# Head norms' statistics in two-block pieces between products, key parts on other engines and in other steps

## The chip, the core and the metric

The kernel runs on one core of a Trainium2 chip. The core has TensorE (PE: matrix products; PEld is the load of a product's stationary operand), VectorE (DVE), ScalarE (ACT), GpSimd (POOL) and SyncE (SP, which issues most transfers). Each engine works through its own queue in order. The metric is the device time of one execution in microseconds (us).

## The reference

Two layers of a decoder trunk over 1024 tokens of width 1024, all float32: a gated short convolution and then sliding-window attention, each followed by a SwiGLU channel mixer. The change lies in the attention layer:

```python
qkv = h @ w_qkv
q = rmsnorm(q, q_gain)      # per head of 64, over 16 query heads
k = rmsnorm(k, k_gain)      # per head of 64, over 4 key heads
scores = einsum(qb, kw) * scale          # 128 queries against 256 keys
scores = where(mask, scores + alibi, -inf)
p = softmax(concat([scores, sink]))[..., :-1]
out = einsum(p, vw)
return out @ w_o
```

## The kernel before

Float32 accuracy is made from a high part (float32r) and a low part (the rest): each product of two matrices is three matrix products, high by high, high by low, low by high. The projections to queries and keys use a seven-product scheme: each pair of 128-column blocks is made from seven sums of products (kinds 0 to 6), and each kind is 12 matmuls of 128x512 (four steps p of three). "Seven kinds of the keys" (numbers j = 0 to 6 in `seq`) are followed by seven of the first query pair (j = 7 to 13); all 14 are run by `first_pairs` before the attention. The remaining query pairs are run piecemeal inside the attention by `work_of_pairs`.

After its last kind a block of raw keys or queries (two heads by 1024 tokens, in a tile of 128 x 1024) is normed. ACT squares it in two halves (`squares`, L2011 for keys, L2134 for queries). PE then sums the squares over each head: `head_stats` (L1678) is one matmul for each 128 tokens, 128 columns of squares as the stationary operand against two columns of ones, so eight for a block of 1024 tokens; as float32 each is two loads and two matmuls in the trace, 16 in all. Their 16 columns go to one PSUM bank. From it DVE makes the mean (`head_mean`, L1685), ACT takes a logarithm and an exponential (L1697, L1702), DVE refines it (L1704 to L1711), ACT or POOL spreads the 16 columns to 128 x 512 (`spread`, L1803), PE turns those (`turn_blocks`, L1808, four matmuls), and DVE multiplies them in (L2036 for keys, L1813 for queries). The bank named P3 serves the statistics and every turn in `first_pairs`; there is one buffer of it, so a turn waits until DVE has read the one before.

The normed keys are then laid out as scores need them: `part(g, e, i)` for key block g and head e makes in four steps a high part (i = 0, ACT, L1873), its copy on the other 64 partitions (i = 1, DVE, L1875), a low part (i = 2, raw minus high, POOL, and DVE for g, e = 0, 0 alone; L1878), and its copy (i = 3, ACT, L1880). Each works on 64 x 1024 elements. The values are scaled and split by `keep_v` (ACT L1794, DVE L1796).

The attention runs in steps, one for 128 tokens of one pair of heads. Within a step the order is written as a string, `ORDER = "SPTMEDkPHLVOPK"`: scores of block n (S; PE, L2231 and L2232, into the bank P0, of which there is one), row extremes (M; DVE, L2246, which read P0), exponentials (E; ACT, L2266, block n-1), turn (T; PE, L2274, block n-2), high and low part of the turned block (H, ACT, L2281; L, DVE, L2287), values (V; PE, L2300, block n-3), their keeping (O; ACT L2318, DVE L2319), and at each P a piece of the products L1997 of a later query pair. At k and K the helpers run that `plan(d, f)` has put d steps ahead: an integer d at K (end of the step), a half at k. `keep_q` plans the norm of one query block in this way: squares at 1 and 1.5, statistics and mean at 2.5, log and refinement at 3, spreading from 3, turns at 4.5 and 5.5. A turn T uses the banks P1 and P3 by turns, and the statistics sit in the one that the next T will take. In `first_pairs` the order is set by a list of due times instead: `line.work` puts PE's work in a row, and `at(t, f)` puts another engine's step at a planned time.

## Time and profile before

| | us |
|---|---|
| median of 3 runs | 1926.59 |
| the runs | 1924.79, 1926.59, 1926.68 |
| the profiled execution, its own time | 1926.32 |
| its span in the trace | 1924.2 |
| PE busy | 1913.0 (99%) |
| DVE, ACT, POOL busy | 1327.0, 893.7, 303.8 |
| chain that ended last, share of PE | 95% |

A line of the timeline merges equal instructions in a row; the start of the next line, not the length, tells how long a group held PE, since PE's matmuls overlap. The stretches that matter lie between 975 us (the first key product) and 1060 us (the attention's twelfth step).

### The profile page before, as it was taken

The page shows a single profiled execution, that of the slowest core. Times are in us where ns is not written, and L with a number is a line of the kernel's source. Part 1 is how long each engine was busy: PE and PEld are TensorE (multiplying, and loading weights), DVE is VectorE, ACT ScalarE, POOL GpSimd, SP SyncE. Part 2 cuts the span into 40 slices and gives each one's busy share as a digit, 9 for nine tenths or more (in the row PEclk, how much of TensorE's full clock was granted, in tenths as well). Part 3 has the DMA queues.
Part 4 walks back from the last instruction along what each step waited for, and adds up shares of the span by engine and source line. Part 5 has one row for each costly group of instructions (what it writes and reads, how often), then busy time and mean ns, then how long its engine had stood idle before and what let it go on. Part 6 is the DMA issues. An engine that isn't in the chain of part 4 may idle for free.

```text
span 1924.2 us, 25416 instructions
## 1 busy us (share of the span) xinstructions
PE 1913.0 (99%) x9045; PEld 1597.5 (83%) x9045; DVE 1327.0 (69%) x2295; ACT 893.7 (46%) x1753; POOL 303.8 (16%) x389
## 2 busy tenths in 40 slices
PE   9999999999999999999999999999999999999999
PEld 8888888888888888888887888888888888888887
DVE  8997877975655666555867987788756665665543
ACT  5543464633333334444557787655333333344441
POOL 0001131011111100000014556310111111100000
PEclk9999999999999999999999999999999999999999
DMA  8896595388898637986364661232675575467563
GB/s 315 260 259 155 117 248 160 112 273 216 221 251 234 154 136 288 320 255 209 105 255 146 210 213 54 89 142 81 218 210 142 197 194 162 131 244 275 197 228 100
DMA packets 154910, 374.13 MB, mean 194 GB/s; under 512 B 15392, under 2 KB 26784, under 8 KB 154784
## 3 DMA queue, kind: packets, MB, share of 16 engines
q1 hardware_dynamic: 119392, 263.16, 39.8%
q0 software_dynamic: 35248, 109.33, 23.1%
q8 instruction: 71, 1.16, 0.2%
q14 instruction: 55, 0.45, 0.1%
q10 hardware_dynamic: 144, 0.03, 0.0%
HBM read 300.89 MB, written 149.42 MB: 234 GB/s over the span
## 4 chain that ended last, share of the span: by engine, by line
PE 95%; DVE 2%; ACT 2%; issue 1%; POOL 0%; DVEq 0%; ACTq 0%; POOLq 0%
PE acc L1004 16%; PE acc L1007 16%; PE acc L1005 16%; PE P L1004 10%; PE P L1005 10%; PE P L1007 10%; PE acc L172 2%; PE P L1997 2%; PE acc L1997 2%; PE acc L176 1%; PE P L2274 1%; PE P L1678 1%; PE acc L1137 1%; PE acc L1139 1%; PE acc L1138 1%
## 5 line engine op out<-in xcount | busy, mean ns | idle before, releaser
L1004 PE MATMUL acc<-XS,G 128*128 128x512 f32 x926 | 360.4, 389 | 0.0
L1005 PE MATMUL acc<-XS,G 128*128 128x512 f32 x926 | 360.2, 389 | 0.0
L1007 PE MATMUL acc<-XS,G 128*128 128x512 f32 x926 | 360.2, 389 | 0.0
L1004 PE MATMUL P<-A,G 128*128 128x512 f32 x550 | 214.1, 389 | 0.0
L1007 PE MATMUL P<-A,G 128*128 128x512 f32 x550 | 214.0, 389 | 0.0
L1005 PE MATMUL P<-A,G 128*128 128x512 f32 x550 | 214.0, 389 | 0.0
L1007 PEld LDWEIGHTS acc<-XS,G 128*128 128x128 f32 x926 | 173.8, 188 | 36.1
L1004 PEld LDWEIGHTS acc<-XS,G 128*128 128x128 f32 x926 | 173.8, 188 | 36.1
L1005 PEld LDWEIGHTS acc<-XS,G 128*128 128x128 f32 x926 | 173.8, 188 | 35.9
L1004 PE MATMUL acc<-A,G 128*128 128x512 f32 x442 | 172.1, 389 | 0.0
L1007 PE MATMUL acc<-A,G 128*128 128x512 f32 x442 | 172.0, 389 | 0.0
L1005 PE MATMUL acc<-A,G 128*128 128x512 f32 x442 | 171.9, 389 | 0.0
L938 DVE TENSOR_TENSOR G<-WL,G 128x512 fp32r<-128x512 f32 x168 | 115.0, 685 | 73.1 <-ACT G L937 73.1
L938 DVE TENSOR_TENSOR G<-WR,G 128x512 fp32r<-128x512 f32 (+1 forms) x216 | 144.2, 668 | 30.7 <-ACT G L937 30.6
L937 ACT CAST G<-WR 128x512 fp32r<-128x512 f32 (+1 forms) x216 | 130.5, 605 | 68.8 <-PE acc L1007 24.6
L937 ACT CAST G<-WH 128x512 fp32r<-128x512 f32 (+1 forms) x174 | 104.7, 602 | 83.8 <-PE acc L1007 38.1
L938 DVE TENSOR_TENSOR G<-WH,G 128x512 fp32r<-128x512 f32 (+1 forms) x174 | 115.5, 664 | 21.6 <-ACT G L937 21.6
L1339 ACT ACTIVATE G<-G 128x512 f32<-128x512 f32 x88 | 55.8, 634 | 159.4 <-DVE G L1436 153.1
L1007 PEld LDWEIGHTS P<-A,G 128*128 128x128 f32 x550 | 103.2, 188 | 21.5
L1004 PEld LDWEIGHTS P<-A,G 128*128 128x128 f32 x550 | 103.2, 188 | 21.4
L1005 PEld LDWEIGHTS P<-A,G 128*128 128x128 f32 x550 | 103.2, 188 | 21.4
L901 POOL DMA_DIRECT2D s<-s x68 | 60.0, 893 | 351.7 <-DMA s<-s 169.6
(414 smaller groups left out, 3797.9 us busy)
## 6 DMA issues: line engine op xcount, KB each, us to landing
G<-h SPq DMA_DIRECT2D x70, 512.0 KB, 4.5
s<-in_w_dn SPq DMA_DIRECT2D x32, 704.0 KB, 8.4
h<-X POOLq DMA_DIRECT2D x44, 512.0 KB, 5.7
s<-s POOLq DMA_DIRECT2D x32, 704.0 KB, 6.9
WR<-s SPq DMA_DIRECT2D x79, 256.0 KB, 4.0
WR<-in_w_gu SPq DMA_DIRECT2D x36, 512.0 KB, 5.5
WH<-in_w_gu SPq DMA_DIRECT2D x36, 512.0 KB, 4.6
XS<-q_ops SPq DMA_DIRECT2D x36, 512.0 KB, 5.0
```

Of the source, the lines that this page charges most:

```text
L172: pe.matmul(ps.half(h), wh, xs[:, j, c], start=first and j == 0, stop=False)
L176: pe.matmul(ps.half(h), wl, xs[:, 0, c], start=False, stop=last)
L901: nc.gpsimd.dma_start(dst[to], dst[of], accum_op=ALU.add)
L937: lambda: act.copy(out_hi, raw),
L938: lambda: lo_eng.tensor_tensor(out_lo, raw, plain(out_hi), ALU.subtract),
L1004: pe.matmul(ps, w[:, 0, c], x[:, 0, :], start=start and e == 0, stop=False, skip_group_check=True)
L1005: pe.matmul(ps, w[:, 0, c], x[:, 1, :], start=False, stop=False, skip_group_check=True)
L1007: pe.matmul(ps, w[:, 1, c], x[:, 0, :], start=False, stop=last, skip_group_check=True)
L1137: pe.matmul(ps, hi[:, kc], xs[:, 0, c], start=k == 0, stop=False, skip_group_check=True)
L1138: pe.matmul(ps, hi[:, kc], xs[:, 1, c], start=False, stop=False, skip_group_check=True)
L1339: state["silu"] = act.activation(x, x, AF.Silu)
L1997: pe.matmul(ps, g[:, w, c], x[:, b, :], start=begin and i == 0, stop=end and i == 2, skip_group_check=True)
```

## The change

Three things change. First, `head_stats` is called for two or four blocks of 128 tokens instead of eight: for the two key blocks and the first query block in four pieces of two, each behind three or six products; for the seven later query blocks in two pieces of four, one at k and one at K of the same step, and the mean goes to K, log, refinement and the first spread half a step later. The second turn of the second key block goes from behind one group of six products to behind the next. Second, of the four key parts, the copy of the high part (i = 1) goes from DVE to ACT (but for the first), the low part (i = 2) from POOL to DVE, and parts 1 to 3 start a step or half a step later. Third, the last two blocks of values are scaled in step 3 instead of step 0. Lines after the change are up to five higher than before (L1878 is L1879, L2036 is L2038, L2246 is L2251).

```diff
@@ part
                 if i == 0:
                     act.copy(hi[rows, e, :], raw[rows, :])
+                elif i == 1 and (g, e) == (0, 0):
+                    dve.tensor_copy(hi[rest, e, :], raw[rows, :])
                 elif i == 1:
-                    dve.tensor_copy(hi[rest, e, :], raw[rows, :])
+                    act.copy(hi[rest, e, :], raw[rows, :])
                 elif i == 2:
-                    eng = dve if (g, e) == (0, 0) else pool
-                    eng.tensor_tensor(lo[rows, e, :], raw[rows, :], plain(hi[rows, e, :]), ALU.subtract)
+                    dve.tensor_tensor(lo[rows, e, :], raw[rows, :], plain(hi[rows, e, :]), ALU.subtract)
@@ first_pairs
-            def stats(g):
-                s["st", g] = bank("P3")
-                head_stats(s["st", g], s["side", g], 0, NB)
+            def stats(g, b):
+                if ("st", g) not in s:
+                    s["st", g] = bank("P3")
+                head_stats(s["st", g], s["side", g][:, b * P : (b + 2) * P], b, 2)
...
+                    if (j, p) in ((5, 1), (5, 2), (5, 3), (6, 0)):
+                        stats_work(0, 2 * (p - 1) % NB)
                     if p == 1 and j == 7:
                         rows_work(0, 0)
-                    if p == 1 and j == 8:
-                        stats_work(1)
-                    if p == 1 and j == 10:
-                        rows_work(1, 1)
-                    if p == 1 and j == 12:
-                        line.work(4, first.stats)
-                        for d, f in ((0.1, first.mean), (0.5, first.guess), (0.9, first.newton), (1.2, first.wide0), (2.9, first.wide1)):
+                    if (j, p) in ((8, 1), (8, 2), (8, 3), (9, 0)):
+                        stats_work(1, 2 * (p - 1) % NB)
+                    if j == 10 and p in (1, 3):
+                        rows_work(1, p // 2)
+                    if (j, p) in ((11, 2), (11, 3), (12, 1), (12, 2)):
+                        line.work(1, first.stats, {(11, 2): 4, (11, 3): 6, (12, 1): 0, (12, 2): 2}[j, p])
+                    if (j, p) == (12, 2):
+                        for d, f in ((0.1, first.mean), (0.3, first.guess), (0.5, first.newton), (0.65, first.wide0), (2.9, first.wide1)):
...
-                if j == 5:
-                    stats_work(0)
-                if j in (7, 9):
-                    rows_work(*{7: (0, 1), 9: (1, 0)}[j])
+                if j == 7:
+                    rows_work(0, 1)
...
-            for pair in (0, 1):
-                at(t + 0.1, keep_v, 1, pair)
+            at(t + 0.1, keep_v, 1, 0)
@@ keep_q
-                (1.5 + first, [stats_of, mean]),
-                (2 + first, [guess, newton]),
-                (rows[0] - 1.5, [lambda: wide_of(0)]),
+                (1.5 + first, [lambda: stats_of(0, 4)]),
+                (2 + first, [lambda: stats_of(4, 4), mean]),
+                (2.5 + first, [guess, newton, lambda: wide_of(0)]),
@@ the attention's steps
-            for d, g, e in ((4, 0, 1), (6.5, 1, 0), (8, 1, 1)):
-                for i, dd in enumerate((0, 0, 0.5, 3.5 if g == 0 else 3)):
+            plan(3, lambda: keep_v(1, 1))
+            for d, g, e in ((5, 0, 1), (7, 1, 0), (8.5, 1, 1)):
+                for i, dd in enumerate((0, 0.5, 1, 3 if g == 0 else 2.5)):
```

DVE's queue at the norm of the second key block (raw keys G_1164), before the first query product's sums (L1979): the first key part's cast and subtraction and the multiplication by the turned factors. Before:

```order
L1711 SCALAR_TENSOR_TENSOR hr_y_8238<-hr_t_8244,hr_y_8238 128x16
L1875 CAST A_1177_8272<-G_1161_8073 64x1024
L2036 SCALAR_TENSOR_TENSOR G_1164_8153<-G_1164_8153,cst_61,P_1175_8265 128x512
L1878 TENSOR_TENSOR A_1178_8273<-G_1161_8073,A_1177_8272 64x1024
L2036 SCALAR_TENSOR_TENSOR G_1164_8153<-G_1164_8153,cst_61,P_1179_8285 128x512
L1979 TENSOR_TENSOR G_1176_8270<-P_1145_7852,G_1176_8270 128x512
```

After the change the same place of DVE's queue reads:

```order
L1711 SCALAR_TENSOR_TENSOR hr_y_8250<-hr_t_8256,hr_y_8250 128x16
L1875 CAST A_1176_8269<-G_1161_8073 64x1024
L1879 TENSOR_TENSOR A_1177_8270<-G_1161_8073,A_1176_8269 64x1024
L2038 SCALAR_TENSOR_TENSOR G_1164_8156<-G_1164_8156,cst_61,P_1178_8278 128x512
L2038 SCALAR_TENSOR_TENSOR G_1164_8156<-G_1164_8156,cst_61,P_1179_8292 128x512
L1980 TENSOR_TENSOR G_1175_8267<-P_1145_7852,G_1175_8267 128x512
```

The subtraction (L1878, now L1879) stood between the two multiplications of the second key block; now it stands ahead of both.

DVE's queue at the attention's first two steps: scaled values (L1796), a weight's split (L1940, L1941) and the row extremes of the first scores (L2246). Before:

```order
L1796 SCALAR_TENSOR_TENSOR A_1192_8402<-acc_7900,r_7999,A_1192_8402 128x4x64 x2
L1796 SCALAR_TENSOR_TENSOR A_1192_8402<-acc_7949,r_7999,A_1192_8402 128x4x64 x2
L1940 CAST WL_7846<-WR_7842 128x512
L1941 TENSOR_TENSOR WL_7846<-WR_7842,WL_7846 128x512
L2246 ISA s_1188_8369,mx_8468<-P_1201_8461,cst_61 128x64
L2246 ISA mx_8468 128x1
L2246 ISA s_1188_8369,mx_8468<-P_1201_8461,cst_61 128x128
L2246 ISA mx_8468 128x1
L1875 CAST A_1177_8272<-G_1161_8073 64x1024
```

After the change DVE's queue reads there:

```order
L1796 SCALAR_TENSOR_TENSOR A_1192_8402<-acc_7900,r_7999,A_1192_8402 128x4x64 x2
L1941 CAST WL_7846<-WR_7842 128x512
L1942 TENSOR_TENSOR WL_7846<-WR_7842,WL_7846 128x512
L1796 SCALAR_TENSOR_TENSOR A_1192_8402<-acc_7949,r_7999,A_1192_8402 128x4x64 x2
L2251 ISA s_1188_8369,mx_8468<-P_1201_8461,cst_61 128x64
L2251 ISA mx_8468 128x1
L2251 ISA s_1188_8369,mx_8468<-P_1201_8461,cst_61 128x128
L2251 ISA mx_8468 128x1
L1941 CAST WL_7847<-WR_7842 128x512
L1942 TENSOR_TENSOR WL_7847<-WR_7842,WL_7847 128x512
```

The second pair of scaled values now stands behind the split, still ahead of the first extremes; the key part's cast behind the extremes is gone.

DVE's queue some steps on, from the turned block's low part (L2287) over the extremes of the fourth scores to the mean of the next query block (L1685). Before:

```order
L2287 TENSOR_TENSOR G_1208_8518<-P_1207_8508,G_1208_8518 128x256
L1940 CAST WL_7846<-WR_7842 128x512
L2246 ISA s_1188_8369,mx_8468<-P_1209_8527,cst_61 128x192
L2246 ISA mx_8468 128x1
L2246 ISA s_1188_8369,mx_8468<-P_1209_8527,cst_61 128x192
L2246 ISA mx_8468 128x1
L1875 CAST A_1211_8543<-G_1164_8153 64x1024
L1685 SCALAR_TENSOR_TENSOR hr_m_8556<-P_1213_8547,eps_r_8000 128x16
L2287 TENSOR_TENSOR G_1216_8561<-P_1210_8534,G_1216_8561 128x512
L2319 TENSOR_TENSOR G_1218_8567<-P_1217_8564,G_1218_8567 64x2x2x64
```

After the change the same steps of DVE's queue read:

```order
L2292 TENSOR_TENSOR G_1208_8517<-P_1207_8506,G_1208_8517 128x256
L1879 TENSOR_TENSOR A_1177_8270<-G_1161_8073,A_1176_8269 64x1024
L1941 CAST WL_7846<-WR_7842 128x512
L2251 ISA s_1188_8369,mx_8468<-P_1209_8527,cst_61 128x192
L2251 ISA mx_8468 128x1
L2251 ISA s_1188_8369,mx_8468<-P_1209_8527,cst_61 128x192
L2251 ISA mx_8468 128x1
L2292 TENSOR_TENSOR G_1212_8549<-P_1210_8534,G_1212_8549 128x512
L2324 TENSOR_TENSOR G_1214_8555<-P_1213_8552,G_1214_8555 64x2x2x64
L1685 SCALAR_TENSOR_TENSOR hr_m_8568<-P_1211_8543,eps_r_8000 128x16
```

A subtraction of a key part (L1879) now stands ahead of the extremes of the fourth scores, a cast behind them is gone, and the mean now stands behind the low part and the kept values instead of ahead of them.

## Rows read from the trace of the kernel before

**Rows 1.** Page, part 1: busy us (share), instructions of each engine.

```profile
PE 1913.0 (99%) x9045; PEld 1597.5 (83%) x9045; DVE 1327.0 (69%) x2295; ACT 893.7 (46%) x1753; POOL 303.8 (16%) x389
```

**Rows 2.** PE timeline, products before the attention: start, us, engine, line, operation, out<-in, count.

```profile
992.08 1.84 PE L1678 MATMUL P<-cst,G 128*128 128x2 f32 x16
...
993.78 2.34 PE L1997 MATMUL P<-A,WH 128*128 128x512 f32 x9
...
998.01 0.60 PE L1808 MATMUL P<-cst,G 128*128 128x128 f32 x4
...
998.36 1.63 PE L1997 MATMUL P<-XS,G 128*128 128x512 f32 x6
...
1007.56 0.60 PE L1808 MATMUL P<-cst,G 128*128 128x128 f32 x4
...
1013.93 1.52 PE L1997 MATMUL P<-A,WL 128*128 128x512 f32 x6
...
1015.54 1.95 PE L1678 MATMUL P<-cst,G 128*128 128x2 f32 x16
```

**Rows 3.** Windows: length, busy us of PE, PEld, DVE, ACT, POOL; clock; DMA; GB/s.

```profile
1017.40:1021.20 3.80, 3.80 (x11) 2.98 (x11) 1.16 (x6) 2.05 (x6) 0.00 (x0) 0.55 0.00 0
...
1032.00:1040.00 8.00, 6.11 (x39) 5.13 (x39) 6.82 (x23) 5.25 (x17) 2.61 (x2) 1.00 0.74 272
...
1040.00:1060.00 20.00, 19.20 (x127) 16.34 (x127) 16.45 (x49) 18.53 (x50) 14.04 (x10) 1.00 0.26 79
```

**Rows 4.** DVE timeline, same stretch; in brackets idle before it, releaser.

```profile
1008.20 0.75 DVE L2036 SCALAR_TENSOR_TENSOR G<-G,cst,P 128x512 f32<-128x512 f32 x1 [0.15 <-PE P L1808]
...
1009.33 1.22 DVE L1878 TENSOR_TENSOR A<-G,A 64x1024 fp32r<-64x1024 f32 x1 [0.38 <-ACT A L1873]
...
1017.52 0.17 DVE L1685 SCALAR_TENSOR_TENSOR hr_m<-P,eps_r 128x16 f32<-128x16 f32 x1 [0.40 <-PE P L1678]
```

**Rows 5.** ACT timeline, same stretch.

```profile
1008.24 1.05 ACT L1873 CAST A<-G 64x1024 fp32r<-64x1024 f32 x1
...
1014.85 0.63 ACT L2134 ACTIVATE G<-G 128x512 f32<-128x512 f32 x1 [1.33 <-DVE G L1981]
...
1018.99 0.62 ACT L1803 COPY G<-hr_y 128x512 f32<-128x512 f32 x1 [0.80 <-DVE hr_y L1711]
```

**Rows 6.** PE timeline of the attention's first steps: the rows with a wait.

```profile
1032.85 0.36 PE L2231 MATMUL P<-A,G 128*128 128x192 f32 x1 [2.25 <-DVE mx L2246]
...
1035.98 0.36 PE L2231 MATMUL P<-A,G 128*128 128x192 f32 x1 [1.04 <-DVE mx L2246]
...
1044.86 0.36 PE L2231 MATMUL P<-A,G 128*128 128x192 f32 x1 [0.19 <-DVE mx L2246]
...
1049.60 0.63 PE L1808 MATMUL P<-cst,G 128*128 128x128 f32 x4 [0.18 <-DVE G L2287]
...
1054.57 0.30 PE L2231 MATMUL P<-A,G 128*128 128x64 f32 x1 [0.43 <-POOL G L2169]
```

**Rows 7.** DVE timeline around the attention's first scores.

```profile
1027.44 1.65 DVE L1796 SCALAR_TENSOR_TENSOR A<-acc,r,A 128x256 fp32r<-128x256 f32 x4
...
1029.53 2.67 DVE L1941 TENSOR_TENSOR WL<-WR,WL 128x512 fp32r<-128x512 f32 x1
...
1032.83 1.05 DVE L1875 CAST A<-G 64x1024 fp32r<-64x1024 f32 x1
```

**Rows 8.** POOL timeline, same stretch as Rows 7.

```profile
1026.87 1.29 POOL L2169 TENSOR_TENSOR G<-G,G 64x512 fp32r<-64x512 f32 x1 [1.69 <-ACT G L2164]
...
1029.27 2.39 POOL L1878 TENSOR_TENSOR A<-G,A 64x1024 fp32r<-64x1024 f32 x1 [1.11 <-ACT A L1873]
```

**Rows 9.** View of line L1875 from 985 to 1180: durations min/median/max in ns.

```profile
L1875 DVE CAST A<-G x4: 689/1000/1648, 1006.4 to 1046.0; 64x1024 fp32r<-64x1024 f32 x4
```

**Rows 10.** Timeline of PE and DVE behind the fourth query block's statistics.

```profile
1085.70 0.62 PE L1997 MATMUL acc<-WH,WL 128*128 128x512 f32 x2
...
1086.52 0.43 DVE L2319 TENSOR_TENSOR G<-P,G 64x256 f32<-64x256 f32 x1
```

More of the change, by code (lines that the diff above doesn't have):

```diff
@@ L2045, in of_product, with stats_work @@
                 all_of(three(j, p, x))
-            def stats_work(g):
-                line.work(4, stats, g)
+            def stats_work(g, b):
+                line.work(1, stats, g, b)
                 t = line.end
+                if b < NB - 2:
+                    return
                 at(t + 0.1, log, g)
@@ L2134, in squares, with stats_of @@
                 act.activation(t["side"][h], t["raw"][:, h * 512 : h * 512 + 512], AF.Square)
-            def stats_of():
-                t["st"] = bank(pos["free"])
-                for h in (0, 1):
-                    head_stats(t["st"], t["side"][h], 4 * h, 4)
+            def stats_of(b0, n):
+                if "st" not in t:
+                    t["st"] = bank(pos["free"])
+                for b in range(b0, b0 + n, 2):
+                    head_stats(t["st"], t["side"][b // 4][:, b % 4 * P : (b % 4 + 2) * P], b, 2)
             def mean():
@@ L2178, in keep_q @@
                     squares0=lambda: squares(0),
-                    stats=stats_of,
+                    stats=lambda b: stats_of(b, 2),
                     mean=mean,
```

## Prediction, made before the changed kernel ran

> **What bounds the kernel now.** I read the page first: PE is busy for 1913.0 us, 99% of the span [rows 1], so any gain must come from time in which PE waits, runs slower or does work of another kind. Then I went through PE's timeline for starts that come later than the work before them explains, from the first key product (975 us) to the end of the attention's first twelve steps (1060 us), where all moved instructions stand. There are three kinds.
>
> The first is the statistics. Sixteen loads and matmuls hold PE from 992.08 to 993.78, 1.70 us, although their matmuls have two columns [rows 2]: one load each, 0.106 us. Ten blocks are normed in this way.
>
> The second is one slow stretch. The first query block's statistics start at 1015.54. The six products from 1013.93 show 1.52, with the last one 0.39 long, so one starts (1.52 - 0.39) / 5 = 0.227 after another, and the next start was due at 1015.29; ACT's squares end at 1014.85 + 0.63 = 1015.48 [rows 2, 5]: a wait of 0.25 us. Right behind these statistics the granted clock is 0.55 for 3.80 us [rows 3], that is 1.2 GHz for nearly all of it and 2.4 GHz elsewhere. At full clock its work takes 3.80 x 0.55 = 2.09, so 1.71 us are lost. What PE did before it fell is the wait and then 1.7 us of two-column matmuls. From 1032 to 1060, with one more such block, it is 1.00 [rows 3].
>
> The third is waits in the attention: 2.25, 1.04, 0.19, 0.18 and 0.43 us [rows 6]. The first has its cause in DVE: a subtraction of 128x512 takes 2.67 us and ends 0.54 us after a POOL subtraction of 2.39 us does [rows 7, 8]. DVE stood still while POOL ran; its own work is near the 0.54. The 1.04 has the key part's cast (1.05) in the way of the next extremes [rows 7].
>
> **The change part by part.** The sum is made against the profiled execution, 1926.32 (2.1 over its span, 0.27 below the median of 1926.59).
>
> *Pieces, PE's own time: 0.* A turn of four matmuls also has four loads, and already stands between products: 0.35 us from 998.01 to 998.36, and the six products behind it last 1.63, about 0.1 over their usual [rows 2]. So four loads cost 0.45 and four pieces 1.8, what one row of sixteen costs with its own 0.1. Bounds: -0.9 (three quartered blocks at 4 x 0.35 against 1.70) to +0.2. The Trainium skill, "TensorE: Matmul & The Clock Gate", section "Architectural detail: the array is 16x 32x32, not 1x 128x128", says that PE can pull weight loads ahead of matmuls in flight. By it the loads of a piece could all hide behind the products beside them; that is the last rival below.
>
> *The wait of 0.25 and the slow clock: -0.25 and -1.71.* In four pieces no more than 0.45 us of two-column work stand together, with 0.7 to 1.4 us of products between. I take the whole; bound 0, if the clock falls elsewhere.
>
> *Second turn of the second key block: +1.08, new.* DVE's subtraction (1.22) now stands ahead of both multiplications. It waits for ACT's part of 64x1024, which started at 1008.24 and took 1.05 [rows 5]; ACT now spreads factors first, 0.53 to the next start (0.62 long) [rows 5], so the part ends near 1009.80, the subtraction runs to 1011.05 [rows 4], and the first multiplication (0.75) to 1011.72. The turned factors of the second half need the same bank P3. PE ends the product before at 1007.56 [rows 2], runs six products (1.36), the first turn (0.44) and six products, and wants the second turn near 1010.7. It gets the bank near 1011.77. Bounds 0 (if ACT or DVE gets there a microsecond earlier) to 1.3.
>
> *Two follow-on waits: +0.23 and +0.27.* From 1011.77 on the multiplication, the kept sum and the squares (0.63) follow each other and end near 1014.45; PE asks for the first piece at 1014.25. The last piece then ends near 1018.96. From the mean's start to the end of the spread before were 1017.52 to 1018.99 + 0.62 = 2.09 [rows 4, 5], with 0.17 for the way to DVE, so 1021.22; PE is at the turn at 1021.0. Here the old order had 1.7 us to spare. Bounds 0 to 0.8.
>
> *First scores: the wait goes from 2.25 to 1.28, -0.97.* POOL no longer has its 2.39 in the way, but its third low part of the queries (1.29) [rows 8] moves up into that place, and starts as DVE comes to the cast and subtraction. So I let DVE stand about 1.2 us again instead of 2. The second pair of scaled values still runs ahead of the extremes (four took 1.65) [rows 7]. Bounds: -2.15 (no meeting) to 0.
>
> *Steps 4 to 12: +0.6.* The waits there were 1.84 (1.04 + 0.19 + 0.18 + 0.43). ACT was idle 2.75 us of the 8 and 1.47 of the 20 [rows 3], 4.22 together; it gets three casts and one first part more in there, 4 x 1.05 = 4.2. It is full, so the stretch can't become shorter by what DVE gives back. DVE loses three casts (0.69 at their shortest [rows 9]; up to 1.05 as they ran) and gets three subtractions of 1.22: 3.66 - 2.07 = +1.59, or +0.97 by casts that waited. Each stands ahead of the extremes of the next scores or of the multiplication that frees a turn's bank, and PE has one bank for scores. DVE had 28 - 23.27 = 4.73 us idle [rows 3], so not all of it lands on the path: two thirds of 0.97. ACT's logarithm now waits for the mean behind a later statistics half, with casts around it, which fills the same 4.22. Bounds: -1.84 (every wait gone) to +2.9 (1.59 and one POOL operation of 1.29 in the way).
>
> *Later blocks (seven in halves): 0.* Two halves hold as many loads. DVE's and ACT's work there is the same, and stands in a step with no statistics wait in the trace. The new tie is a rival.
>
> Sum: -0.25 - 1.71 + 1.08 + 0.50 - 0.97 + 0.60 = -0.75, so 1925.57, 0.05% below the median before. About 0.2%, 3.85 us, is what a measurement of this kernel can tell from no change: 1922.7 to 1930.4.
>
> **The rivals.**
>
> *The queues take the new work.* ACT and DVE were idle for 4.2 and 4.7 us in the stretch, and a due-time order may meet well: no new turn waits, DVE never meets POOL, all 1.84 gone: -0.25 - 1.71 - 2.15 - 1.84 = -5.95, 1920.4. Against it: ACT has nothing left, and three waits would have to vanish together. Half of it gives 1922 to 1923.
>
> *The mean holds up the turn.* With the statistics at K, the next T takes their bank and must wait until DVE has read the mean. Behind the fourth block: products end at 1085.70 start plus 0.46, then half the statistics 0.88, scores 0.45, one product 0.23, so T at 1087.72; DVE's kept values end at 1086.95 [rows 10], the mean follows the statistics (1087.04) near 1087.4. 0.3 us to spare: it decides where DVE is later than that. With one low part and one kept block more ahead (0.69 + 0.43) T waits 0.8; seven blocks, 5.6: 1925.57 + 5.6 = 1931.2, slower. For it: DVE was busy 23.27 of 28 us. Against: nothing but the mean moved there, and low parts may start earlier, since ACT no longer waits for 1.7 us of statistics first.
>
> *The clock is not given back.* A wait of 1.08 between two turns may bring the low clock as 0.25 and statistics did: 1925.57 + 1.71 = 1927.3, no change. For it: the timed runs before differ by 1.8, about one such stretch, so it comes in some executions and not in others.
>
> *The pieces' loads hide behind the products* (the rule above): ten blocks of 1.70, 17 us, 1909. Against: the turn of four loads at 998.01 still costs 0.35 [rows 2].
>
> **How the numbers follow.** Forecast 0.57 (1924 to 1927); queues take the work 0.20; the mean holds up the turn 0.07; the clock is not given back 0.15; loads hide 0.01. Faster: most of the first rival, and the last: 0.18. Slower: most of the second: 0.06. Same: 0.76. The range leaves out the better half of the first rival and the second: 1921.9 to 1928.2.
>
> **What would show it.** Right: no window below clock 1.00 near 1017; statistics in groups of four with starts 0.45 apart from their products; a PE wait near 1 us at the second key block's second turn, on DVE; a first scores wait of 1 to 1.5; ACT busy over 95% from steps 4 to 10, and PE waits of 2 to 3 us in sum there, on DVE. Wrong: no wait at that turn, or less than 1 us of waits in steps 4 to 12 (then 1920 to 1923); turns that wait for a mean in the later blocks (then 1928 and more).

## The result, and the profile of the changed kernel

The changed kernel takes 1929.52 us (median of 12, 1928.79 to 1934.50); the kernel before takes 1926.09 beside it (12, 1924.79 to 1927.14). The medians are 3.43 us (0.18%) apart. The ratio is 1.0023, 95% interval [1.0014, 1.0032]; it lies nearer to that of the means (1930.62 and 1926.11) than to that of the medians. So the kernel is slower clear of noise, by about the 0.2% that the prediction named as its limit. The ratios here and below leave out three disturbed executions of later runs (2751.55, 3910.2 and 4834.2 us). Forecast were 1925.57 and 1921.9 to 1928.2. The profiled execution took 1929.86, its span 1928.1.

First the page's part 1 and then four windows of the changed kernel, with the columns of [rows 1] and [rows 3]:

```profile
PE 1915.2 (99%) x9045; PEld 1598.3 (83%) x9045; DVE 1326.9 (69%) x2295; ACT 896.5 (46%) x1756; POOL 296.8 (15%) x386
```

```profile
1017.00:1021.00 4.00, 4.00 (x23) 3.33 (x21) 1.66 (x7) 1.74 (x6) 0.00 (x0) 1.00 0.00 0
...
1040.00:1047.00 7.00, 6.57 (x25) 5.82 (x26) 5.12 (x16) 4.71 (x14) 2.16 (x3) 0.53 0.11 39
1047.00:1060.00 13.00, 11.02 (x71) 8.92 (x69) 11.43 (x30) 11.91 (x27) 4.85 (x4) 1.00 0.14 50
...
1032.00:1060.00 28.00, 25.17 (x143) 21.05 (x141) 21.23 (x59) 24.10 (x55) 7.29 (x7) 0.88 0.33 115
```

There is no slow clock near 1017 [rows 3]. A longer one stands in the attention: 0.53 of full speed from 1040 to 1047. The stretch behind it has PE idle for 2 us of 13, though its clock is full. PE's timeline has the waits, those of the key products first:

```profile
1011.65 0.63 PE L1808 MATMUL P<-cst,G 128*128 128x128 f32 x4 [0.91 <-DVE G L2038]
...
1031.33 0.36 PE L2236 MATMUL P<-A,G 128*128 128x192 f32 x1 [1.15 <-DVE mx L2251]
...
1036.90 1.05 PE L1678 MATMUL P<-cst,G 128*128 128x2 f32 x8 [0.20 <-DVE G L2292]
...
1040.43 0.50 PE L2236 MATMUL P<-A,G 128*128 128x192 f32 x1 [0.65 <-DVE mx L2251]
...
1054.10 0.63 PE L2279 MATMUL P<-cst,G 128*128 128x128 f32 x4 [0.98 <-DVE WH L1813]
...
1055.24 0.38 PE L2305 MATMUL P<-G,A 128*128 128x256 f32 x1 [0.28 <-ACT G L2286]
1055.96 0.38 PE L2306 MATMUL P<-G,A 128*128 128x256 f32 x1 [0.34 <-DVE G L2292]
...
1057.43 0.27 PE L2236 MATMUL P<-A,G 128*128 128x64 f32 x1 [0.38 <-DVE mx L2251]
```

The same work can be followed through both traces (times from the span's start):

| place on PE | before | after | gained or lost since the row above | the prediction's terms for it |
|---|---|---|---|---|
| first key product | 975.73 | 975.44 | | |
| first scores | 1028.85 | 1028.43 | -0.13 | -0.25 - 1.71 + 1.08 + 0.50 = -0.38 |
| next scores, which have the wait of 2.25 in [rows 6] | 1032.85 | 1031.33 | -1.10 | -0.97 |
| first scores of the second query block | 1054.57 | 1057.43 | **+4.38** | +0.60 |
| scores of a later step | 1154.62 | 1157.85 | +0.37 | 0 |
| end of the span | 1924.2 | 1928.1 | +0.67 | 0 |

The first two stretches came out near the forecast; the third decides, with steps 4 to 12. But the -0.13 is luck in good part. Seven of the experiments below (e2, e7, e9, e10, e11, e14 and e15) have the first three norms just as the kernel before has them. In their traces PE is busy for the same 13.91 us from 1010 to 1024, and the clock is full in all seven. The kernel before, then e11:

```profile
1010.00:1024.00 14.00, 13.91 (x64) 11.29 (x64) 7.10 (x16) 8.32 (x17) 3.42 (x9) 0.88 0.31 106
```

```profile
1010.00:1024.00 14.00, 13.91 (x73) 11.50 (x73) 7.23 (x17) 9.73 (x21) 4.61 (x9) 1.00 0.35 117
```

In the seven the first scores stand 51.51 to 51.56 us after the first key product, against 53.12 in the kernel before and 52.99 in the changed one. So the slow clock near 1017 came in the one execution that was profiled, and went without any change to the statistics: that the pieces remove it is not shown. Against an execution at full clock the change loses 1.4 to 1.5 us here instead of gaining 0.13.

The last row's loss lies in one place: the eighth block's statistics start at 1180.33 in place of 1176.37. In DVE's and ACT's timelines ahead of the wait at 1054.10 stand:

```profile
1051.67 1.56 DVE L1879 TENSOR_TENSOR A<-G,A 64x1024 fp32r<-64x1024 f32 x1
1053.26 0.69 DVE L1813 TENSOR_TENSOR WH<-WH,P 128x512 f32<-128x512 f32 x1
```

```profile
1051.45 1.05 ACT L1881 CAST A<-A 64x1024 fp32r<-64x1024 f32 x1
1053.32 1.26 ACT L2169 CAST G<-WH 64x512 fp32r<-64x512 f32 x2 [0.82 <-DVE A L1879]
1054.60 0.59 ACT L2286 CAST G<-P 128x512 fp32r<-128x512 f32 x1
```

The fourth key part's subtraction runs ahead of the multiplication (L1813) that frees a turn's bank, so the turn waits 0.98. And ACT waits 0.82 for the subtraction, because its first parts of the next query block (L2169) go into the buffer G4 that holds the raw keys which the subtraction reads (`key_raw[1]` and `Q[1]` are both in G4). The cast of the next turned block (L2286), the values (L2305, L2306) and the scores queue up behind it.

The waits of this stretch, from the second scores of the table to those of the second query block, sum to 2.83 us, where the kernel before has 1.84. In this one execution most of the +4.38 is therefore the low clock, 6.8 us at half speed. Whether the change would cost less without it is told by the executions at full clock, below.

### The profile page after: what moved, and what is told of

Read it like the earlier page. It is cut to its first block, busy times and chain, and to the rows that moved or that the text cites. A ratio compares the mean times of both kernels' runs of the same rounds, so it can differ in the third digit from the quotient of the medians.

```text
span 1928.1 us, 25403 instructions
## 1 busy us (share of the span) xinstructions
PE 1915.2 (99%) x9045; PEld 1598.3 (83%) x9045; DVE 1326.9 (69%) x2295; ACT 896.5 (46%) x1756; POOL 296.8 (15%) x386
## 3 DMA queue, kind: packets, MB, share of 16 engines
q8 instruction: 71, 1.16, 0.2%
## 4 chain that ended last, share of the span: by engine, by line
PE 94%; DVE 3%; ACT 2%; issue 1%; DMA 0%; POOL 0%; DVEq 0%; ACTq 0%; POOLq 0%
PE acc L1007 16%; PE acc L1004 16%; PE acc L1005 16%; PE P L1004 10%; PE P L1005 10%; PE P L1007 10%; PE acc L172 2%; PE P L1998 2%; PE acc L1998 2%; PE acc L176 1%; PE P L2279 1%; PE acc L1137 1%; PE acc L1139 1%; PE acc L1138 1%; PE P L1678 1%
## 5 line engine op out<-in xcount | busy, mean ns | idle before, releaser
L937 ACT CAST G<-WL 128x512 fp32r<-128x512 f32 x168 | 103.3, 616 | 24.4 <-DVE WL L886 12.9
```

Source lines behind the costliest of these rows:

```text
L937: lambda: act.copy(out_hi, raw),
```

## The experiments

Theory 1 was that the change slows PE through the clock: the halves thin out its products and the low clock comes where there was none. Theory 2 was that in the attention's first steps DVE and ACT set the pace, so that the changed queues cost the time. Medians in us, with that of the kernel before beside them and the difference ("less before"). A run whose interval holds 1 can't be told from the kernel before by its time.

| run | on which kernel, what | median | before | less before | ratio [95%] |
|---|---|---|---|---|---|
| e1_whole_later | changed, later halves undone | 1929.45 | 1926.49 | +2.96 | 1.0015 [1.0006, 1.0024] |
| e2_halves_alone | before, halves only | 1927.86 | 1926.49 | +1.37 | 1.0007 [0.9998, 1.0016] |
| e3_parts_back | changed, parts undone | 1928.60 | 1926.49 | +2.11 | 1.0016 [1.0007, 1.0025] |
| e4_pieces_alone | before, pieces only | 1928.56 | 1926.49 | +2.07 | 1.0013 [1.0004, 1.0022] |
| e5_sub_later | changed, first subtraction later | 1928.48 | 1926.58 | +1.90 | 1.0011 [1.0002, 1.0020] |
| e6_parts_sooner | changed, three parts sooner | 1929.05 | 1926.58 | +2.47 | 1.0012 [1.0003, 1.0021] |
| e7_halves_wide_sooner | e2, spread sooner | 1927.22 | 1926.58 | +0.64 | 0.9999 [0.9991, 1.0008] |
| e8_all_mended | changed, e1 + e5 + e6 | 1926.55 | 1926.58 | -0.03 | 0.9997 [0.9989, 1.0006] |
| e9_parts_alone | before, parts only | 1928.34 | 1926.50 | +1.84 | 1.0008 [0.9999, 1.0017] |
| e10_subs_on_dve | before, subtractions on DVE | 1927.13 | 1926.50 | +0.63 | 1.0005 [0.9996, 1.0014] |
| e11_casts_on_act | before, casts on ACT | 1926.56 | 1926.50 | +0.06 | 1.0001 [0.9993, 1.0010] |
| e12_pieces_and_one_part | e4 + e5, one subtraction on DVE | 1925.37 | 1926.50 | -1.13 | 0.9995 [0.9986, 1.0004] |
| e13_e12_with_casts | e12 and casts on ACT | 1926.26 | 1927.29 | -1.03 | 0.9996 [0.9988, 1.0005] |
| e14_engines_alone | before, both engines, old steps | 1927.02 | 1927.29 | -0.27 | 0.9997 [0.9988, 1.0006] |
| e15_steps_alone | before, later steps, old engines | 1930.87 | 1927.29 | +3.58 | 1.0020 [1.0011, 1.0029] |
| e16_steps_back | changed, old steps | 1930.34 | 1926.40 | +3.94 | 1.0016 [1.0007, 1.0025] |
| e17_three_mended | e16 + e5 + e1 | 1925.20 | 1926.40 | -1.20 | 0.9994 [0.9985, 1.0002] |

### Which third of the change

e1 makes the later statistics whole again; e2 puts the halves alone into the kernel before:

```diff
-                (1.5 + first, [lambda: stats_of(0, 4)]),
-                (2 + first, [lambda: stats_of(4, 4), mean]),
-                (2.5 + first, [guess, newton, lambda: wide_of(0)]),
+                (1.5 + first, [lambda: stats_of(0, 8), mean]),
+                (2 + first, [guess, newton]),
+                (rows[0] - 1.5, [lambda: wide_of(0)]),
```

> The changed kernel, with the statistics of all later query blocks whole again, at the place they had before. Theory (the halves thin out PE's products where DVE makes it wait, and the clock falls there): no stretch under clock 0.9 between 1036 and 1050, 3.4 us less than the changed kernel's 1929.5, so about 1926.1. Rival 1 (the key parts on ACT and DVE cost the time by waits, and the low clock follows from them): 1929 to 1930, slow stretches still there. Rival 2 (the pieces in the key products cost it): 1929 to 1930.

> The kernel before, with the later blocks' statistics in halves and nothing else. Theory in its strong form (halves alone bring the low clock): one or two slow stretches behind block 1's statistics, 1926.1 + 1.7 to 3.4 = 1927.8 to 1929.5. Theory in its weak form (it takes the halves and the new waits on DVE together): 1926.1, clock 1.00 from 1036 to 1050. Rivals 1 and 2: 1926.1.

e3 takes the part change back (engines, steps and `keep_v`); e4 and e9 make the pieces alone and the parts alone (with `keep_v`) in the kernel before, out of the hunks of the diff shown ahead.

> The changed kernel, with the key parts and the last values on the engines and at the steps they had before; pieces and halves stay. Theory, strong form: the slow stretches stay, the new waits of about 2.1 us go, near 1927.5. Weak form: both go, near 1924 to 1925.5. Rival 1: both go, near 1924 to 1925.5. Rival 2: 1929 to 1930.

> The kernel before, with the first three norms' statistics in pieces and the turned factors of the second key block at their new places, nothing else. By the terms of the sum: -1.96 for the wait and the slow clock near 1017, +1.08 for the new wait at the second turn, +0.34 for the two waits that follow, so 1925.5, with clock 1.00 from 1017 to 1021 and a first scores wait of 2.25 as before. Rival 2: 1927 to 1930.

> The kernel before with the key parts and the last values on the engines and at the steps of the changed kernel, nothing else. By the prediction's terms: first scores -0.97, steps 4 to 12 +0.60, so 0.4 less than before, 1926.2. By the runs so far (changed kernel less the one with the parts back, 1.3; pieces with parts less pieces alone, 0.9): 0.9 to 1.3 more than before, 1927.5 to 1927.9, with waits of DVE's multiplication and of what follows near the ninth step, 2 us in sum.

Theory 1 fell with e1: it has whole statistics, its clock is still 0.81 from 1040 to 1048, and it is still 2.96 slower. Each third alone costs by its median, 2.07, 1.37 and 1.84, together 5.3, while the whole change costs 3.4: they meet at the same waits and hide one another. (The intervals of e2 and e9 just hold 1.) e9 has the parts' waits by themselves (1.16 at the first scores; 1.07 for L1813, 0.29 and 0.34 near the ninth step), where the terms said a gain of 0.4. e3, without them, keeps a cost of 2.11. The executions say the same in another way, since each also has its mean granted clock. Of the changed kernel five show 1.000, and these take 1928.8 to 1929.2. Of the kernel before (beside e1 to e4) four show 1.000, with a mean of 1924.8. At full clock throughout, then, the change costs 4.2 us; the low clock is not what it is slower by. Where the clock is full, PE comes to the waits sooner and stands there longer: e5 below, traced at full clock, waits 3.95 us in steps 4 to 12 where the changed kernel's trace has 2.83.

e4's second scores no longer wait 2.25, and the next ones take that back. DVE, PE and POOL of e4:

```profile
1030.38 2.17 DVE L1875 CAST A<-G 64x1024 fp32r<-64x1024 f32 x1
1032.57 1.38 DVE L1940 CAST WL<-WR 128x512 fp32r<-128x512 f32 x1
```

```profile
1035.60 0.36 PE L2236 MATMUL P<-A,G 128*128 128x192 f32 x1 [3.09 <-DVE mx L2251]
```

```profile
1029.15 2.84 POOL L1878 TENSOR_TENSOR A<-G,A 64x1024 fp32r<-64x1024 f32 x1 [0.77 <-ACT A L1873]
...
1032.07 1.60 POOL L2174 TENSOR_TENSOR G<-G,G 64x512 fp32r<-64x512 f32 x1
```

In the kernel before, POOL's subtraction met DVE's subtraction (2.67 us, a wait of 2.25) [rows 6 to 8]. In e4 DVE's subtraction starts at 1029.05, 0.10 ahead of POOL's, takes 0.69, and the wait of 2.25 is down to 0.25. Then the cast meets the same POOL operation and takes 2.17 where it can take 0.69 [rows 9]. The next scores wait 3.09 in place of 1.04: the price is POOL's, and it only changed its payer.

### Inside the parts: engines or steps

e10 sets `dve.tensor_tensor` for all subtractions, e11 `act.copy` for the three later casts, at the old steps; e14 does both; e15 has only the later steps, with the last values in step 3. (The last values were not moved by themselves in any run.)

```diff
-            for d, g, e in ((4, 0, 1), (6.5, 1, 0), (8, 1, 1)):
-                for i, dd in enumerate((0, 0, 0.5, 3.5 if g == 0 else 3)):
+            plan(3, lambda: keep_v(1, 1))
+            for d, g, e in ((5, 0, 1), (7, 1, 0), (8.5, 1, 1)):
+                for i, dd in enumerate((0, 0.5, 1, 3 if g == 0 else 2.5)):
```

> The kernel before, with the three later subtractions of 64x1024 on DVE instead of GpSimd, at their old steps, nothing else. If the cost of the parts is DVE's 1.22 each in the queue ahead of extremes and multiplications: 1 to 2 us more than before, 1927.6 to 1928.6. If what counts is that DVE stands still beside GpSimd's 2.4 to 2.7 us of each (so DVE loses nothing by doing it itself): same or up to 1.5 us less, 1925 to 1926.6, and the first scores' wait of 2.25 falls to about 1.3.

> The kernel before, with the three later casts of 64x1024 (rest rows) on ACT instead of DVE, at their old steps, nothing else. If ACT is full in steps 4 to 12: waits for ACT's casts or copies appear on PE or behind DVE, 0.5 to 1.5 us more than before, 1927.1 to 1928.1. If ACT has room: 0 to 1 us less (DVE's casts of 1.05, 0.95 and 0.69 no longer stand ahead of the extremes), 1925.6 to 1926.6.

> The kernel before with both engines of the key parts changed (casts on ACT, subtractions on DVE), all at their old steps, last values as before. If the engines make the cost of the parts (1.84 alone): 1928 to 1928.5. If the later steps make it: the two edits added, 1926.5 + 0.6 + 0.1 = 1927.2 or less, and no wait for the multiplication near the ninth step.

> The kernel before with the key parts at their later steps and the second half of the last values later, all on their old engines. If the later steps make the cost: 1927.5 to 1928.3, with a wait for DVE's multiplication near the ninth step, 1 us or more. If the engines make it: 1926 to 1927, since GpSimd's subtraction stays and no DVE work is added; the first scores' wait of 2.25 then falls, since GpSimd's subtraction comes a step later.

With the old engines the steps cost 3.58; the engines alone cost -0.27, nothing that can be told. At each mean clock that both show (0.997 to 0.999) e14 averages 0.4 to 1.2 us below the kernel before. All waits of PE from 1008 to 1062 in e14 are one row of the view of waits (sum, times, longest):

```profile
PE P L2232 <- DVE mx L2247: 2.7, 3, 1.7
```

That is less than the 4.09 of [rows 6], though a clock of 0.79 from 1040 to 1048 may hide some of them there; together with the times it says that ACT did have room for the casts and DVE for the subtractions. In e15 the raw keys' buffer shows at its worst. POOL, ACT and PE:

```profile
1051.04 2.36 POOL L1878 TENSOR_TENSOR A<-G,A 64x1024 fp32r<-64x1024 f32 x1
```

```profile
1053.43 1.26 ACT L2163 CAST G<-WH 64x512 fp32r<-64x512 f32 x2 [4.46 <-POOL A L1878]
1054.71 0.59 ACT L2280 CAST G<-P 128x512 fp32r<-128x512 f32 x1
```

```profile
1055.35 0.38 PE L2299 MATMUL P<-G,A 128*128 128x256 f32 x1 [2.98 <-ACT G L2280]
```

ACT stands for 4.46 us until POOL has read the raw keys, with the turned block's cast behind it, and PE waits 2.98. At its old place the last subtraction is issued a step sooner, and in the kernel before neither ACT's L2164 nor PE waits for it there [rows 6]. The expected wait for L1813 did not come in e15. Another of its waits, 1.93 at 1044.90, is not the buffer's: a cast of 64x1024 on DVE meets POOL's subtraction at the new step. DVE and POOL:

```profile
1041.34 2.70 DVE L1875 CAST A<-G 64x1024 fp32r<-64x1024 f32 x1
```

```profile
1041.12 2.36 POOL L1878 TENSOR_TENSOR A<-G,A 64x1024 fp32r<-64x1024 f32 x1
```

In the changed kernel neither operation runs on that engine at this place, so e15 alone overstates what the steps cost there. With the new engines they cost about 2.1 (e9 at +1.84 against e14 at -0.27, measured at different times). Of e10 and e11 each, alone, too little is seen to tell it from nothing; in e10 the wait of 2.25 is 0.64, but a later one is 2.24.

### The second turn, the mean and the spread

e5 lets the first part's subtraction come behind both multiplications; e6 makes the three other parts sooner; e7 puts the guess, the Newton step and the first spread right behind the mean, in e2:

```diff
-                    for i, d in enumerate((0.7, 0.06, 1.6, 3.1)):
+                    for i, d in enumerate((0.7, 0.06, 3.9, 5.4)):
...
-            for d, g, e in ((5, 0, 1), (7, 1, 0), (8.5, 1, 1)):
+            for d, g, e in ((4.5, 0, 1), (6, 1, 0), (7, 1, 1)):
...
-                (2 + first, [lambda: stats_of(4, 4), mean]),
-                (2.5 + first, [guess, newton, lambda: wide_of(0)]),
+                (2 + first, [lambda: stats_of(4, 4), mean, guess, newton]),
+                (rows[0] - 1.5, [lambda: wide_of(0)]),
```

> The changed kernel, with the subtraction of the first key part issued behind the two multiplications of the second key block (and the cast that follows it later too). Both theories: the wait of 0.91 at the second turn falls to about 0, and the first scores stand about 1 us earlier. Theory 1 (PE's own waits in the key products decide): the end comes 1.1 to 1.4 us earlier, 1928.2. Theory 2 (from the first scores on, DVE and ACT set the pace; what PE gains ahead of them is lost at their waits): 1929.5 still, within 0.5, and the waits of the first steps grow by what was gained.

> The changed kernel, with the second, third and fourth key parts half a step, one step and one and a half steps sooner, so that no subtraction of 64x1024 stands ahead of a multiplication that frees a turn's bank in steps 8 to 10. Theory 2 (DVE's queue): the wait of 0.98 for DVE's multiplication near 1054 goes, with it most of the three that follow it (0.28, 0.34, 0.38); the scores of the second query block come 1.5 to 2.3 us earlier, about 1927.5. Rival (ACT is full there, whatever stands where): the four waits only move, 1929 to 1930.

> The kernel before with halves, and the guess, the Newton step and the first spread right behind the mean in the same step instead of half a step later. Theory (the halves cost by the later spread: POOL's spread comes later, POOL's sink subtraction behind it too, ACT waits 1.07 for that in place of 0.33, and PE 0.89 in place of 0.19 at the eighth block's statistics): that wait is 0.2 to 0.3 again and 0.6 to 0.75 come back of what the halves alone cost, 1926.1 to 1927.2. Rival (two pieces with products between them cost PE by themselves, or the bank is held longer): the wait stays, 1927.5 to 1928.

e5's second turn no longer waits (its row), and in its profiled execution the clock of 1040 to 1047 is full, as it is in five of the changed kernel's twelve:

```profile
1011.31 0.60 PE L1808 MATMUL P<-cst,G 128*128 128x128 f32 x4
```

```profile
1040.00:1047.00 7.00, 5.82 (x37) 4.45 (x36) 5.16 (x18) 6.58 (x16) 1.16 (x2) 1.00 0.10 37
```

By the medians it recovers about 1.5 of the 3.4, as theory 1 of its expectation said; between executions at a mean clock of 1.000 it recovers 0.6 (1928.4 against 1929.0), between the two theories. PE is busy for only 5.82 of those 7 us, and it still waits 1.07 at L2279 for L1813. Those waits need no low clock. One more, 0.69 at L1808 for POOL's spread (L1803), belongs to the halves: e1, with whole statistics, does not have it.

e6 removed that wait and got another, since the second part's subtraction now stands ahead of the mean, and the turn needs the mean's bank. PE and DVE:

```profile
1042.74 1.09 PE L2279 MATMUL P<-cst,G 128*128 128x128 f32 x4 [2.25 <-DVE hr_m L1685]
```

```profile
1041.18 1.21 DVE L1879 TENSOR_TENSOR A<-G,A 64x1024 fp32r<-64x1024 f32 x1
1042.42 0.17 DVE L1685 SCALAR_TENSOR_TENSOR hr_m<-P,eps_r 128x16 f32<-128x16 f32 x1
```

This is the rival of the prediction, at another place. e7 answers for the eighth block. POOL, ACT and PE, first of the kernel before and then of e2:

```profile
1165.77 0.22 POOL L2329 TENSOR_TENSOR mx<-mx,cst 128x16 f32<-128x16 f32 x1
...
1166.01 0.22 ACT L2330 ACTIVATE mx<-mx 128x16 f32<-128x16 f32 x1 [0.33 <-POOL mx L2329]
...
1176.37 1.95 PE L1678 MATMUL P<-cst,XS 128*128 128x2 f32 x16 [0.19 <-DVE G L2287]
```

```profile
1163.25 0.61 POOL L1803 COPY G<-hr_y 128x512 f32<-128x512 f32 x1 [1.93 <-PE P L2233]
...
1165.62 0.21 POOL L2330 TENSOR_TENSOR mx<-mx,cst 128x16 f32<-128x16 f32 x1
...
1165.87 0.21 ACT L2331 ACTIVATE mx<-mx 128x16 f32<-128x16 f32 x1 [1.07 <-POOL mx L2330]
...
1175.82 1.05 PE L1678 MATMUL P<-cst,XS 128*128 128x2 f32 x8 [0.89 <-DVE G L2288]
```

With the spread (L1803) half a step later, POOL's small subtraction for the division comes later too, ACT waits 1.07 for it in place of 0.33, and ten us on PE waits 0.89 in place of 0.19. In e7 these are 0.33 and 0.42, and e7 costs 0.64 where e2 costs 1.37. The two medians' spreads overlap (e2 1925.60 to 1931.68, e7 1925.06 to 1927.62), so the waits show it rather than the times.

### Within the changed kernel, and all together

e16 puts the old steps of e15's diff back into the changed kernel, and `keep_v` too; e8, e12, e13 and e17 join edits already shown (e12 and e13 take DVE for the second part's subtraction alone).

> The changed kernel with the key parts at their old steps and both halves of the last values at their old place; the new engines, the pieces and the halves stay. If the later steps cost the time (3.6 alone, engines alone nothing): the wait for DVE's multiplication near the ninth step and the two behind it go, and the time falls by 1.5 to 3 us, to 1926.5 to 1928. If it was the sum of work on ACT and DVE: 1929 to 1930.

> The changed kernel with the statistics of later blocks whole, the first subtraction behind the multiplications, and the three key parts sooner. If the three costs add up and none is lost at DVE and ACT: 1929.5 - 0.5 - 1.2 - 2 = 1925.8, at or below the kernel before. If DVE and ACT set the pace from the first scores on: about 1927.

> The kernel before, with the pieces in the key products, the first subtraction behind the two multiplications, and the second key part's subtraction (the one that meets DVE before the first scores) on DVE; all other parts as before. If the cause of the loss is named rightly (the wait at the second turn, and the meeting of DVE with GpSimd's subtraction at the first scores): the first two waits there sum to 1.5 us or less in place of 3.3, and the time is 0.5 to 2 us below before, 1924.6 to 1926.1. If DVE and ACT set the pace anyhow: 1926.6, within 0.5.

> The kernel of the pieces with one subtraction on DVE, and the three later casts of 64x1024 on ACT as well. If DVE's casts ahead of the extremes cost and ACT has room (the casts alone showed neither gain nor loss in the time, but waits of 0.32 and 0.31 in place of 1.04 and 0.19): 0.3 to 1 us less than its 1925.4, so 1924.4 to 1925.1. If ACT is full: 1925.4 to 1926.5.

> The same, with the first subtraction behind the two multiplications and the later statistics whole too: what is left of the change is the pieces in the key products and the new engines. If the three places named (second turn, later steps, later spread) are the whole loss: at or below the kernel before, 0.5 to 1.5 us less, like the kernel with one subtraction moved (1.1 less). If something of the loss is unnamed: 0.5 us or more above before.

e16 missed as a time and hit in part as a trace. The wait for L1813 near 1054 and the two behind it are gone. Its first scores of the second query block stand at 1055.26, in place of 1057.43, with the first key product near 975.43 in both: 2.2 gained, 1.3 if the stretch is compared with e5's at full clock (23.78 us against 25.06). What is left there, against 21.72 in the kernel before, are mostly waits of the halves, for the mean and for the spread that follows it:

```profile
1042.11 0.63 PE L2280 MATMUL P<-cst,G 128*128 128x128 f32 x4 [1.26 <-DVE hr_m L1685]
...
1045.94 0.66 PE L1808 MATMUL P<-cst,G 128*128 128x128 f32 x4 [0.69 <-POOL G L1803]
```

As a time, 4 executions took 1927.4 to 1928.1 and 7 took 1930.2 to 1931.8, with a mean clock of 1.000 or 0.999 in the four and 0.998 or 0.997 in the seven. The profiled one is of the seven. Windows of e16 and of the changed kernel:

```profile
1180.00:1187.00 7.00, 7.00 (x31) 6.36 (x30) 3.45 (x13) 2.15 (x8) 0.61 (x1) 0.53 0.01 3
```

```profile
1180.00:1187.00 7.00, 6.67 (x47) 6.17 (x48) 5.83 (x21) 3.99 (x15) 2.47 (x4) 1.00 0.12 40
```

Behind the wait of 0.93 for the eighth block's statistics, their first half, four products and four value matmuls, e16's clock is at half for nearly 7 us; in the changed kernel's profiled execution the same wait and halves leave it full. So a low clock comes here in some executions and not in others. It does not need the halves: in e8 and e9, whose statistics are whole, the clock is 0.80 and 0.82 from 1175 to 1183. Between executions at 1.000 e16 takes 1928.0 against the changed kernel's 1929.0, so the old steps alone give back 1.0 of the 4.2.

e8 comes out even with the kernel before: e6's order has the wait for the mean. In e12 the first two waits are 0.65 and 0.68, 1.33 in place of 3.29, and it takes 1.13 less than the kernel before, with an interval that still holds 1; the casts on ACT add nothing to that (e13).

e17 keeps the pieces and the new engines, with the old steps, the subtraction later and whole statistics. It takes 1925.20, ratio 0.9994 [0.9985, 1.0002], against 1.0023 for the changed kernel: put right together, the three places account for the whole loss. One by one they give back less (e5 0.6 and e16 1.0 at full clock, e1 nothing that can be told), which fits that what one frees is lost at the next. Its five executions at 1.000 average 1924.55, the kernel before's four 1924.84. It has the lowest median of all versions, but the intervals of both comparisons, with the kernel before and with e12's 0.9995, leave no difference to tell. The waits of e17 from 1030 to 1062:

```profile
PE P L2237 <- DVE mx L2252: 1.9, 2, 1.3
PE P L1808 <- DVE G L2293: 0.6, 1, 0.6
PE P L2237 <- POOL G L2175: 0.3, 1, 0.3
```

## Why the prediction was wrong, step by step

- *Pieces at no cost: right.* The pieces start 0.47 or 0.37 ahead of the product behind them (1014.39 to 1014.86, 1015.63 to 1016.00), as the 0.45 said. In e17, where the second turn does not wait, the first scores stand 51.92 us after the first key product, 0.36 to 0.41 over the seven traces with whole statistics, and the two follow-on waits below make up nearly all of it.
- *The wait of 0.25 and the slow clock, -1.96: this term failed too.* It took the price from one execution that had the low clock. The seven traces with whole statistics have the same wait and the same row of sixteen matmuls (in e2 from 1015.14) and are at full clock there. So the low clock was not their standing price, and the pieces are not shown to remove it. Its size in that one execution was right (53.12 against 51.5 us, 1.6). The kernel before takes 1924.8 in executions at full clock and 1926.5 in the median, so by the medians 1.65 is all that a full clock everywhere could bring. The near hit of the first stretch rests on this.
- *Second turn +1.08: right.* 0.91 idle, 1.07 from start to start, on DVE's L2038. Six traces with this wait have 52.94 to 53.02 us from the first key product to the first scores, five without it 51.86 to 51.92. The two follow-on waits were 0.19 and 0.15 (forecast 0.23 and 0.27); e5 and e17 have them without the wait, so they come with the pieces' places.
- *First scores 1.28: right.* 1.31 from start to start, and DVE's subtraction took 1.59 beside POOL's third low part, as told.
- *Steps 4 to 12, +0.6: this step failed.* It measured +4.4, beyond the bound of +2.9, and still +3.3 in e5, where the clock is full (25.06 us from the second scores to those of the second query block, 21.72 before). The sum of the waits, 2.83, lies in the 2 to 3 that the prediction named as its sign, but by luck: the low clock hid more of them. ACT, said to be full at over 95%, was busy for 24.10 of 28 us, 86%. The prediction compared ACT's idle 4.22 with the added 4.2 and DVE's idle with the added 0.97, that is, amounts of work. e14 shows that the amounts cost nothing; e15, and e16 against the changed kernel, show that the steps do. Not all of the +3.3 is theirs: with the old steps (e16, full clock there) +2.1 is left, with whole statistics and the subtraction later as well (e17) +0.6. So the halves' later mean and spread share in it; the prediction named them here and gave them no price. What stands behind the fourth part at its new step was never walked: the multiplication for a turn's bank was named, but not that the next block's parts wait for the same raw keys' buffer, with the turned block's cast queued on ACT behind them.
- *Later blocks in halves, 0: wrong by 0.7 at the eighth block, besides their share in steps 4 to 12.* The spread that moved half a step was not walked along POOL's queue. The 0.37 ahead of that block lies in several small waits and was not followed further.
- *Rivals.* "The mean holds up the turn" did not happen in the later blocks; e6 and e16 show its mechanism at block 1 (2.25 and 1.26). "The clock is not given back" was right in kind, since the profiled execution has a low clock at another place, but it costs less than its share of lost clock and varies between executions. "The queues take the new work" came true in no run; nearest to it are the engines alone (e14), whose waits fell by 1.4 while the time stayed. "Loads hide" did not happen: a piece holds PE for 0.36 to 0.47 us.

## What to carry to other kernels

When an operation moves to another step, list what it reads and writes and who needs those buffers next: the last read of a buffer that the next block overwrites belongs well ahead of that block, whatever room the engines have. A gain ahead of a stretch that another engine paces can be lost at that engine's first wait, as in e4; look there for the operation that makes it slow, and move or replace that one. Comparing idle time with added work tells whether work fits, not where it will stand. And a price read from one execution with a low clock needs a second trace of the same instructions before it is booked as a gain.

## What the runs showed of the hardware

In this kernel a low clock cost about half of the time that it took, since PE also waits for others. Of the kernel before (beside e1 to e4) fifteen executions with a mean clock of 0.999 average 1925.9 us and six with 0.997 average 1927.9: 1.0 us for each 0.001, though 0.001 of the span is 1.9 us. In the changed kernel 6.8 us at half clock (0.50 from 1039.8 to 1046.6, that is 1.2 GHz), 3.4 lost, delay the second block's first scores by 1.0 against e5, counted from the first key product (81.99 against 79.88 us, 1.07 of it the second turn). The Trainium skill, "TensorE: Matmul & The Clock Gate", section "Terms", puts the penalty at the gated time times the clock's missing share, so 3.4 here; the trace shows that as an upper end: two thirds of it did not come through, and PE's waits in that stretch are 2.83 us in place of e5's 3.95.

DVE's casts stop for POOL as its subtractions do: 64x1024 took 2.17 us in e4 and ended 0.56 after POOL's subtraction did, 128x512 took 1.38 in place of 0.42. The Trainium skill, "SBUF — State Buffer", section "Who interferes with whom", says that whoever comes first gets the port pair shared by DVE and GpSimd for its whole instruction and the other blocks fully, and it names casts among the operations that can; these rows agree.
